# Input tiles first and in a row, decay loads and two sigmoids held back, GLA gate weights in two loads and copies

## The chip, the core and the metric

The kernel runs on one core of a Trainium2 chip. The metric is the device time of one execution in microseconds (us). The engines are TensorE (PE, matrix products, with its own weight loads), VectorE (DVE), ScalarE (ACT), GpSimd (POOL) and SyncE (SP), which only issues DMAs here. ACT issues DMAs as well, from the same queue as its arithmetic.

## What is computed

One step of a two-layer backbone over 128 context tokens and 512 latent tokens of width 1024. Layer 0 mixes with two groups of heads side by side, HGRN2 (4 heads) and GLA (4 heads of key width 64); layer 1 is retention with 8 heads. Every scan runs in both directions.

```python
def rms_norm(x, w):
    y = xf * lax.rsqrt(jnp.mean(xf * xf, axis=-1, keepdims=True) + EPS)
    return (y * w.astype(jnp.float32)).astype(x.dtype)
...
    for l in range(DEPTH):
        sh_c, sc_c, g_c = jnp.split(cond_ctx @ ada_w[l] + ada_b[l], 3, axis=-1)
        ...
        h_c = rms_norm(x_c, norm_w[l]) * (1.0 + sc_c) + sh_c
        h_l = rms_norm(x_l, norm_w[l]) * (1.0 + sc_l) + sh_l
        ...
# layer 0
    p = h @ w_in
    aq, ai, af_f, af_b, ag, bq, bk, bv, bg, bl_f, bl_b = jnp.split(p, EVEN_SPLIT_IDX, axis=-1)
    def log_forget(a):
        return jnp.logaddexp(jnp.log(lbf), jnp.log1p(-lbf) + jax.nn.log_sigmoid(a.astype(jnp.float32)))
    def gla_log_gate(low, d):
        return jax.nn.log_sigmoid((low @ gk_w[d] + gk_b[d]).astype(jnp.float32)) / GLA_GATE_NORM
# layer 1
    lg = jax.nn.log_sigmoid(decay_logit.astype(jnp.float32))
# every head: the scan
    S_t = diag(g_t) S_{t-1} + k_t v_t^T,  o_t = S_t^T q_t
```

`ret_decay` (the decay logits of layer 1), `hgrn_lb` (the lower bounds of layer 0's HGRN gate) and `gla_gk_w` (two 16x256 matrices, one per direction) are the small inputs that the change is about, beside `norm_w`, `gla_gk_b` and `ada_b`.

## The kernel before

**Staging.** PE's order is the order in which the program is written. The other engines' instructions are put in order by the framework's scheduler, except inside a `manual_schedule` block that names their engine, where the written order holds. `issue_after(ins)` keeps the instructions inside it behind `ins` on their engine. The program as built gives its hardware DMAs eight completion semaphores in turn, and a DMA waits in the queue that issues it until the one eight before it has landed.

**Front.** Five token tiles `x0` to `x4` (128x1024; the loads stand at L128 and L509) are normalised, scaled (`x_scaled`), transposed on PE (`pxt`) and copied to `xnt`. `ident` is the identity for transposes. `vrows` holds 76 rows of small vectors that ACT's queue loads in four pieces (L141 to L144 in the changed kernel); transposed and copied they are `vecs`. The adaLN weights of layer 0 come in chunks `ada` (two loads of 512 KB for each of eight steps k); each step k is a run of `pada` products on PE, a copy `arow` on ACT (L259), a transpose `padv` on PE (L89), small DVE operations on `ab`, and then `first_h(k)`, which makes `h0h` (ACT, L491) and `h0l` (DVE, L492), the two fp32 halves of the input of layer 0.

**Weights.** A block of 128x512 fp32 (256 KB) goes through three steps: SP loads `raw` (L171, five buffers), ACT casts it to `wh` (L180, eight buffers), and POOL, or DVE for a few, takes the difference `wl` (L182, eight buffers). `weights(i)` writes these for blocks ahead of use. A full-precision product is three matmuls, of `h` and `l` halves.

**The k loop** (`pbv`, GLA's values) runs over the eight steps k with the five tiles inside; `first_h(k + 1)` and the adaLN step k + 2 are written into it. At k = 5 the tile `gkw` (128x512, the two 16x256 matrices repeated in four row groups at places that depend on the direction) is cleared and loaded, and `wbl` too.

**Behind it.** `plow` (the low-rank projection) is copied by ACT to `low` (L574); `pz`, made with `gkw`, gives the GLA gates through a chain of ACT activations and DVE operations (L755 to L783) to `K` and `Q`, from which PE takes the scores `px`. `lbv` and `clb` are sigmoids of `hgrn_lb` for the HGRN gate. Then come two GLA head rows, with the projection of the HGRN values between them (`ids_ai`; ACT's copies `v`, L796), and the HGRN heads. In a row, ACT copies scores to `A` (L717, L718) and transposed keys to `kt` (L725), PE multiplies `pkv` from `v` and `kt`, and `po` is the output. `decays()` makes the tables of layer 1's decays: loads `lags` and `lag`, two `log_sigmoid` chains on the small tiles `lsb` and `lsr`, and `dk`, `tab`; they are read in layer 1.

Of the kernel before, what the change touches and what calls it, by code (L numbers as in the profile page):

```python
# [19 lines left out]
NT = 5  # L20
# [21 lines left out]
def hybrid_kernel(  # L42
# [20 lines left out]
    def ps(name="ps"):  # L63
        return psp.tile([128, 512], F32, tag="ps", name=name)
# [60 lines left out]

    ident = const.tile([128, 128], F32, name="ident")
    x_t = [tokt(f"x{t}") for t in range(NT)]
    SP.dma_start(x_t[0], x_rows[0])  # L128
    SP.dma_start(ident, k_ident)
    condr = const.tile([16, 128], F32, name="condr")  # L130
    nc.scalar.dma_start(condr[0:8, :], c_ctx.rearrange("(k p) -> k p", p=128))
    nc.scalar.dma_start(condr[8:16, :], c.rearrange("o (k p) -> (o k) p", p=128))
    NV = 76
    O_NW, O_LB, O_GKB, O_AB = (0, 8), 16, 24, (28, 52)
    vrows = const.tile([NV, 128], F32, name="vrows")
    ACTQ = nc.scalar
    ACTQ.dma_start(vrows[0:16, :], norm_w.rearrange("l (k p) -> (l k) p", p=128))
    ACTQ.dma_start(vrows[16:24, :], hgrn_lb.rearrange("l (k p) -> (l k) p", p=128))
    ACTQ.dma_start(vrows[24:28, :], gla_gk_b.rearrange("o d (k p) -> (o d k) p", p=128))
    ACTQ.dma_start(vrows[28:76, :], ada_b.rearrange("l (k p) -> (l k) p", p=128))  # L140
    mask = const.tile([128, 6, 64], U8, name="mask")  # L141
    mhalf = const.tile([128, 1], F32, name="mhalf")
    V.memset(mhalf, -0.5)
# [350 lines left out]
    def x_square(t):  # L494
        return rms(x_t[t], junk)
# [12 lines left out]
    for t in range(1, NT):
        SP.dma_start(x_t[t], x_rows[t])  # L509
    chunks = {0: ada_first(0)}  # L510
    weights(ids_bv[0], 0)
    chunks[1] = ada_first(1)
    weights(ids_bv[1], 0)
    chunks[2] = ada_first(2)
    with tc.manual_schedule(engines={mybir.EngineType.Activation, mybir.EngineType.DVE, mybir.EngineType.Pool}):
        p = ps("pv")
        transpose(p[:, 0:16], condr)
        S.activation(condp[:, :, 0:2], p[:, 0:16].rearrange("p (c k) -> p k c", c=2), AF.Silu)
        transpose(p[:, 128:128 + NV], vrows)
        V.tensor_copy(vecs, p[:, 128:128 + NV])  # L520
        for l in range(2):
            one = vecs[:, O_AB[l] + 8:O_AB[l] + 16]
            V.tensor_scalar(one, one, 1.0, None, op0=ADD)
        r = [x_square(t) for t in range(2)]
        x_scaled(0, r[0])
        for t in range(NT):
            if t + 1 < NT:
                x_scaled(t + 1, r[t + 1])
            if t + 2 < NT:
                r.append(x_square(t + 2))  # L530
            if t == NT - 1:
                fin = ada_first_mm(0, chunks[0])
                next(fin)
            x_turned(t)
        for _ in fin:
            pass
        first_h(0, 0)
        first_h(0, 1)
        fin = ada_first_mm(1, chunks[1])
        next(fin)  # L540
    pv = [ps(f"pbv{t}") for t in range(NT)]
    for k in range(KC):
        wh, wl = weights(ids_bv[k], 1 if k < 6 else LOOK)
        if k + 3 < KC:
            chunks[k + 3] = ada_first(k + 3)
        if k == 5:
            gkw = tokt("gkw")[:, 0:512].rearrange("p (d n) -> p d n", d=2)
            G.memset(gkw, 0.0)
            for gg in range(4):
                for d in range(2):  # L550
                    ACTQ.dma_start(gkw[32 * gg + 16 * d:32 * gg + 16 * d + 16, d, :], gla_gk_w[0, d])
            wbl = tokt("wbl")[:, 0:256].rearrange("p (k n) -> p k n", k=KC)
            ACTQ.dma_start(wbl, w0.rearrange("(k p) n -> p k n", p=128)[:, :, C_BL:C_BL + 32])
        for t in range(NT):
            g, o = group_of(t)
# [70 lines left out]
    def decays():  # L626
        lags = misc.tile([128, 20], F32, tag="lags", name="lags", bufs=1)
        lag = misc.tile([8, 257], F32, tag="lag", name="lag", bufs=1)
        zb, z8 = lags[:, 2:18], lags[0:8, 18:20]
        ACTQ.dma_start(zb, ret_decay.rearrange("o d h -> o (d h)").to_broadcast([128, 16]))  # L630
        ACTQ.dma_start(z8, ret_decay.rearrange("o d h -> (o h) d"))
        ACTQ.dma_start(lags[:, 0:2], k_ramp)
        ACTQ.dma_start(lag[:, 128:257], k_lag[:, 128:257])
        ACTQ.dma_start(lag[:, 0:128], k_lag[:, 257:385])
# [434 lines left out]
```

## Time and profile before

| | before |
|---|---|
| median of 3 runs | 795.43 us (794.30 to 798.55) |
| the profiled execution | 797.16 us |
| its span, first to last instruction | 795.4 us |
| mean granted PE clock, share of full speed | 0.984 |
| PE / DVE / ACT / POOL busy | 758.2 / 428.8 / 334.2 / 289.6 us |

Times of a row of the timeline are a start, counted from the span's start, and a duration. A number in brackets behind a row is the idle time of its engine just ahead of it and what ended it. In windows, x counts the instructions; the clock of 0.50 is 1.2 GHz, of 1.00 2.4 GHz. In the rows, L numbers are lines of the kernel before.

### The profile page before, as it was taken

How to read it: one execution, taken by the hardware profiler on the slowest of the kernel's cores; microseconds unless marked ns; L12 is line 12 of the kernel's file. 1: busy time of each engine (PE TensorE's matmuls, PEld its weight loads, DVE VectorE, ACT ScalarE, POOL GpSimd, SP SyncE). 2: the span in 40 equal slices, each digit the busy share in tenths (PEclk: the TensorE clock that was granted, in tenths of full speed). 3: DMA queues.
4: the chain of work that ended last, by engine and by line, in shares of the span. 5: the costliest groups of instructions: out<-in, count | busy, mean ns of one | idle time of the engine just before them, and what ended most of it. 6: DMA issues, size and time to landing. Idle time of an engine off the chain costs nothing.

```text
span 795.4 us, 15429 instructions
## 1 busy us (share of the span) xinstructions
PE 758.2 (95%) x6116; PEld 664.2 (84%) x6116; DVE 428.8 (54%) x744; ACT 334.2 (42%) x757; POOL 289.6 (36%) x263
## 2 busy tenths in 40 slices
PE   4999789999989899899999999999999999999996
PEld 3768778789889798778888888899999999888885
DVE  4973793752986666663444940036454646324433
ACT  6447643444534444443534552324333332235322
POOL 2261430265552522331344521544443532043221
PEclk9999899999999999999999999999999999999998
DMA  9982432364433431318524432334333333544003
GB/s 292 315 268 92 142 108 62 114 181 126 144 96 107 147 98 38 81 41 265 152 84 145 152 118 87 94 105 106 100 104 90 115 91 94 173 126 133 14 26 133
DMA packets 104776, 98.62 MB, mean 124 GB/s; under 512 B 7660, under 2 KB 80896, under 8 KB 104704
## 3 DMA queue, kind: packets, MB, share of 16 engines
q1 hardware_dynamic: 83520, 82.15, 33.4%
q10 hardware_dynamic: 21184, 15.49, 7.1%
q8 instruction: 48, 0.79, 0.4%
q14 instruction: 24, 0.20, 0.1%
HBM read 86.31 MB, written 8.16 MB: 119 GB/s over the span
## 4 chain that ended last, share of the span: by engine, by line
PE 68%; DVE 8%; issue 2%; ACT 1%; POOL 1%; DMA 1%; ACTq 0%; POOLq 0%; DVEq 0%
PE pt L85 32%; PE pf L85 21%; PE po L85 5%; PE px L85 4%; PE pkv L85 3%; DVE K L695 2%; DVE T L821 1%; DVE T L699 1%; PE pyt L89 1%; PE pada L85 1%; PE pkt L89 1%; DMA rot<-qk 1%; DVE K L819 1%; DVE Q L697 1%; PE pxt L89 1%
## 5 line engine op out<-in xcount | busy, mean ns | idle before, releaser
L182 POOL TENSOR_TENSOR wl<-raw,wh 128x512 fp32r<-128x512 f32 x142 | 203.0, 1444 | 309.4 <-ACT wh L180 264.4
L180 ACT CAST wh<-raw 128x512 fp32r<-128x512 f32 x168 | 103.2, 621 | 97.8 <-PE pf L85 37.0
L85 PE MATMUL pf<-h0h,wh 128*128 128x384 f32 (+1 forms) x256 | 64.1, 332 | 0.0
L335 DVE SCALAR_TENSOR_TENSOR y<-po,rr,gn 128x128 f32<-128x128 f32 x80 | 24.2, 345 | 72.3 <-POOL rr L158 60.5
L85 PE MATMUL pf<-h1h,wh 128*128 128x384 f32 (+1 forms) x256 | 60.3, 317 | 0.0
L85 PE MATMUL pf<-h0l,wh 128*128 128x384 f32 (+1 forms) x256 | 58.9, 311 | 0.0
L85 PE MATMUL pf<-h0h,wl 128*128 128x384 f32 (+1 forms) x256 | 58.6, 310 | 0.0
L85 PE MATMUL pf<-h1l,wh 128*128 128x384 f32 (+1 forms) x256 | 58.3, 309 | 0.0
L85 PE MATMUL pf<-h1h,wl 128*128 128x384 f32 (+1 forms) x256 | 58.3, 309 | 0.0
L687 ACT COPY km<-K 128x640 f32<-128x640 f32 x42 | 32.8, 782 | 56.3 <-DVE K L695 40.8
L85 PE MATMUL pt<-wh,h1h 128*128 128x512 f32 x160 | 53.9, 402 | 0.0
L156 POOL TENSOR_SCALAR rv<-ss 128x3 f32<-128x3 f32 (+1 forms) x32 | 11.0, 345 | 113.0 <-ACT junk L327 111.8
L85 PE MATMUL pt<-wh,h1l 128*128 128x512 f32 x160 | 52.1, 390 | 0.0
L85 PE MATMUL pt<-wl,h1h 128*128 128x512 f32 x160 | 52.0, 390 | 0.0
L697 DVE TENSOR_TENSOR Q<-Q,T 128x640 f32<-128x640 f32 x42 | 40.5, 964 | 19.2 <-PE px L85 19.1
L916 DVE TENSOR_TENSOR qk<-qk,cs 128x1024 f32<-128x1024 f32 x8 | 9.8, 1226 | 74.9 <-DMA rot<-qk 74.9
L695 DVE TENSOR_TENSOR K<-K,T 128x640 f32<-128x640 f32 x42 | 44.8, 1067 | 6.4 <-ACT km L687 5.9
L327 ACT ACTIVATE junk<-po 128x128 f32<-128x128 f32 x80 | 22.3, 278 | 54.0 <-PE po L85 41.7
L85 PEld LDWEIGHTS pf<-h0h,wh 128*128 128x128 f32 x256 | 39.6, 192 | 4.8 <-issue 2.3
L85 PE MATMUL pt<-wh,h0h 128*128 128x512 f32 x120 | 43.7, 429 | 0.0
L85 PEld LDWEIGHTS px<-Q,km 64*64 64x64 f32 (+1 forms) x1120 | 29.9, 139 | 15.7 <-issue 9.7
L85 PE MATMUL px<-Q,km 64*64 64x64 f32 (+1 forms) x1120 | 35.6, 231 | 5.9 <-DVE Q L697 4.8
(219 smaller groups left out, 1702.2 us busy)
## 6 DMA issues: line engine op xcount, KB each, us to landing
raw<-in_w_in_even_dram SPq DMA_DIRECT2D x64, 256.0 KB, 3.0
araw<-in_ada_w_dram SPq DMA_DIRECT2D x64, 256.0 KB, 3.7
raw<-in_w_in_odd_dram SPq DMA_DIRECT2D x64, 256.0 KB, 2.9
ada<-in_ada_w_dram SPq DMA_DIRECT2D x16, 512.0 KB, 6.3
raw<-in_w_out_even_dram SPq DMA_DIRECT2D x24, 256.0 KB, 3.0
rot<-qk ACTq DMA_DIRECT2D x32, 128.0 KB, 3.5
raw<-in_w_out_odd_dram SPq DMA_DIRECT2D x16, 256.0 KB, 3.0
x<-xr SPq DMA_DIRECT2D x5, 512.0 KB, 2.7
```

The lines of the kernel that those rows point to most:

```text
L85: PE.matmul(out, lhsT, rhs, **kw)
L89: PE.transpose(out, in_, ident[0:in_.shape[0], 0:in_.shape[0]])
L156: G.tensor_scalar(v[:, :n], ssum, 1.0 / count, EPS, op0=MUL, op1=ADD)
L180: S.copy(wh, raw)
L182: (V if n in on_dve else G).tensor_tensor(wl, raw, wh.bitcast(F32), op=SUB)
L327: S.activation(junk, p[:, 128 * i:128 * i + 128], AF.Square, accum_out=ss[:, j:j + 1])
L335: V.scalar_tensor_tensor(dst, p[:, 128 * i:128 * i + 128], r[:, j:j + 1], dst if have else gn[:, col:col + 128], op0=MUL, op1=MUL)
L687: S.copy(km.rearrange("p (n b h) -> p n b h", b=2, h=h), ap(kf, 0, ([2 * h, T // (2 * h)], [T + h, 2], [1, h])))
L695: V.tensor_tensor(keys, keys, ap(th, 1, ([nn - 1, 2], [2, nb], [0, h])), op=MUL)
L697: V.tensor_tensor(queries, queries, ap(th, 0, ([nn + 1, 2], [2, nb], [0, h])), op=MUL)
L699: V.tensor_tensor(t2, ap(th, 0, ([nn, 2], [2, nb])), ap(th, 1, ([nn, 2], [2, nb])), op=MUL)
L916: V.tensor_tensor(lat, lat, cos.unsqueeze(1).to_broadcast([128, 2, 512]), op=MUL)
```

## The change

Five edits. The x tiles, `ident` and `condr` are issued at the start inside a manual order for SP, and the four loads of `vrows` go from ACT's queue to SP's, behind them; the transpose of `vrows` goes to just ahead of the last but one x tile. The `ada` and first `raw` loads are in written order too. `gkw` is loaded in two pieces for the first row group, and POOL copies it to the three others. The two sigmoids of `lbv` are kept behind the last `low` copy. The five loads of `decays()` are kept behind the last `v` copy of the HGRN projection; what is worked out from them follows.

```diff
@@ start
-    SP.dma_start(x_t[0], x_rows[0])
-    SP.dma_start(ident, k_ident)
...
+    with tc.manual_schedule(engines={mybir.EngineType.SP}):
+        SP.dma_start(x_t[0], x_rows[0])
+        nc.scalar.dma_start(condr[0:8, :], c_ctx.rearrange("(k p) -> k p", p=128))
+        SP.dma_start(ident, k_ident)
+        nc.scalar.dma_start(condr[8:16, :], c.rearrange("o (k p) -> (o k) p", p=128))
+        for t in range(1, NT):
+            SP.dma_start(x_t[t], x_rows[t])
...
-    ACTQ.dma_start(vrows[0:16, :], norm_w.rearrange("l (k p) -> (l k) p", p=128))
...
+    with tc.manual_schedule(engines={mybir.EngineType.SP}):
+        SP.dma_start(vrows[0:16, :], norm_w.rearrange("l (k p) -> (l k) p", p=128))
...
@@ x tiles
+            if t == NT - 2:
+                pq = ps("pv")
+                transpose(pq[:, 0:NV], vrows)
+                V.tensor_copy(vecs, pq[:, 0:NV])
...
@@ k == 5
             G.memset(gkw, 0.0)
-            for gg in range(4):
-                for d in range(2):
-                    ACTQ.dma_start(gkw[32 * gg + 16 * d:32 * gg + 16 * d + 16, d, :], gla_gk_w[0, d])
+            for d in range(2):
+                ACTQ.dma_start(gkw[16 * d:16 * d + 16, d, :], gla_gk_w[0, d])
+            for gg in range(1, 4):
+                G.tensor_copy(gkw[32 * gg:32 * gg + 32], gkw[0:32])
@@ behind the k loop
-        S.copy(low[:, off:off + n], p[:, :n])
+        last_low = S.copy(low[:, off:off + n], p[:, :n])
...
-    S.activation(clb, lbv, AF.Sigmoid, scale=-1.0)
-    S.activation(lbv, lbv, AF.Sigmoid)
+    with tc.issue_after(last_low.ins):
+        S.activation(clb, lbv, AF.Sigmoid, scale=-1.0)
+        S.activation(lbv, lbv, AF.Sigmoid)
@@ decays
+        with tc.issue_after(copied[-1].ins):
+            ACTQ.dma_start(zb, ret_decay.rearrange("o d h -> o (d h)").to_broadcast([128, 16]))
...
+            ACTQ.dma_start(lag[:, 0:128], k_lag[:, 257:385])
...
     def v_use(t, p):
-        S.copy(v_t[t][:, 0:512], p)
+        copied.append(S.copy(v_t[t][:, 0:512], p))
```

What stands on ACT at the end of the first GLA head row, before the change (`pt` is the product of the values' projection, `px` the scores, `pkt` the transposed keys):

```order
L796 COPY v_752<-pt 128x512
L717 COPY A<-px 64x5x64
L718 COPY A<-px 64x5x64
L717 COPY A<-px 64x5x64
L718 COPY A<-px 64x5x64
L725 COPY kt<-pkt 128x512 x2
L180 CAST wh<-raw 128x512
```

and after it (lines are those of the changed kernel, where L725 and L726 are the `A` copies and L733 the `kt` copies):

```order
L806 COPY v_759<-pt 128x512
L638 DMA lags<-in_ret_decay_dram 128x16
L639 DMA lags<-in_ret_decay_dram 8x2x1
L640 DMA lags<-in_k_ramp_dram 128x2
...
L641 DMA lag<-in_k_lag_dram 8x129
L642 DMA lag<-in_k_lag_dram 8x128
L606 ACTIVATE lsb<-lags 128x16
L607 ACT_TABLE_LOAD
L607 ACTIVATE lsb<-lsb 128x16
L733 COPY kt<-pkt 128x512 x2
L184 CAST wh<-raw 128x512
```

Between the `v` copy and the `kt` copies now stand five DMA issues, two activations and a table load; the four `A` copies, left out here, keep their place between the third and the fourth issue. The second `lag` issue waits for the semaphore of a weight block's `raw` load.

What stands on ACT behind the `low` copies, ahead of GLA's gates, before:

```order
L574 COPY low<-plow 128x256
L574 COPY low<-plow 128x384
L665 DMA S<-in_state_gla_dram 128x128
L755 ACTIVATE Q<-pz,vecs 128x256
L665 DMA S<-in_state_gla_dram 128x128
L755 ACTIVATE Q<-pz,vecs 128x384
```

and after:

```order
L580 COPY low<-plow 128x256
L580 COPY low<-plow 128x384
L589 ACT_TABLE_LOAD
L589 ACTIVATE clb<-lbv 128x4
L763 ACTIVATE Q<-pz,vecs 128x256
L590 ACTIVATE lbv<-lbv 128x4
L763 ACTIVATE Q<-pz,vecs 128x384
```

A table load and the two sigmoids have come in, ahead of and between the first `Q` activations. In the whole program ACT loads a table 18 times instead of 17.

What stands on ACT around k = 5 to 7 of the k loop, before (`pada` is the adaLN product of a step, `xnt` the transposed tiles):

```order
L553 DMA wbl<-in_w_in_even_dram 128x8x32
L180 CAST wh<-raw 128x512
L551 DMA gkw<-in_gla_gk_w_dram 16x256 x4
L491 CAST h0h_111<-xnt_109 128x256
L551 DMA gkw<-in_gla_gk_w_dram 16x256
L491 CAST h0h_113<-xnt_109 128x384
L259 COPY arow<-pada 128x128
L180 CAST wh<-raw 128x512
L551 DMA gkw<-in_gla_gk_w_dram 16x256 x3
L180 CAST wh<-raw 128x512 x3
L491 CAST h0h_111<-xnt_109 128x256
```

and after:

```order
L559 DMA wbl<-in_w_in_even_dram 128x8x32
L184 CAST wh<-raw 128x512
L555 DMA gkw<-in_gla_gk_w_dram 16x256 x2
L495 CAST h0h_121<-xnt_119 128x256
L495 CAST h0h_123<-xnt_119 128x384
L263 COPY arow<-pada 128x128
L184 CAST wh<-raw 128x512 x5
L495 CAST h0h_121<-xnt_119 128x256
L184 CAST wh<-raw 128x512
L495 CAST h0h_123<-xnt_119 128x384
L263 COPY arow<-pada 128x128
```

Two `gkw` issues stand where eight stood, in one place, and five casts instead of four, and a sixth, stand ahead of the last `h0h` and `arow` shown. On POOL the copies stand between the clearing of `gkw` and the next differences:

```order
L553 MEMSET gkw 128x512
L557 COPY gkw<-gkw 32x512 x2
L186 TENSOR_TENSOR wl<-raw,wh 128x512
L557 COPY gkw<-gkw 32x512
L186 TENSOR_TENSOR wl<-raw,wh 128x512 x11
```

Before, the clearing of `gkw` was followed by eleven differences and nothing between.

## Rows read from the trace of the kernel before

**Rows 1.** The page's busy times by engine, of the whole span
```profile
PE 758.2 (95%) x6116; PEld 664.2 (84%) x6116; DVE 428.8 (54%) x744; ACT 334.2 (42%) x757; POOL 289.6 (36%) x263
```

**Rows 2.** Windows: busy us by engine, PE's clock, DMA share, GB/s
```profile
5.00:8.00 3.00, 0.36 (x1) 0.18 (x1) 0.76 (x6) 2.97 (x5) 0.42 (x2) 1.00 0.64 155
...
12.00:28.00 16.00, 14.40 (x164) 10.64 (x167) 14.11 (x50) 9.37 (x26) 4.44 (x7) 1.00 1.13 348
```

**Rows 3.** Waits of SP, 0 to 13 us: us, times, longest
```profile
SPq L509 <- DMA vrows<-in_norm_w_dram: 2.8, 1, 2.8
```

**Rows 4.** Timeline of PE, 19 to 24 us: start, us; in brackets idle before
```profile
19.25 1.07 PE L85 MATMUL pada<-ada,condp 128*32 128x128 f32 x28 [0.94 <-DMA ada<-in_ada_w_dram]
```

**Rows 5.** Timeline of PE, 54.5 to 57 us
```profile
55.20 0.50 PE L85 MATMUL pbv<-wh,h0h 128*128 128x512 f32 x1 [1.07 <-ACT h0h L491]
...
56.58 0.50 PE L85 MATMUL pbv<-wh,h0l 128*128 128x512 f32 x1 [0.88 <-DVE h0l L492]
```

**Rows 6.** Windows in which PE's clock was 0.50
```profile
57.30:60.50 3.20, 3.20 (x10) 2.43 (x9) 2.61 (x4) 0.00 (x0) 1.92 (x2) 0.50 0.62 176
...
238.20:241.40 3.20, 3.20 (x40) 2.50 (x38) 2.99 (x10) 0.05 (x1) 0.00 (x0) 0.50 0.39 93
```

**Rows 7.** Timeline of PE, 236.8 to 240 us
```profile
236.85 2.65 PE L85 MATMUL pkv<-v,kt 128*128 128x128 f32 x16 [2.20 <-ACT kt L725]
```

**Rows 8.** Timeline of ACT, 65 to 69 us
```profile
65.47 2.02 ACT L755 ACTIVATE Q<-pz,vecs 128x384 f32<-128x384 f32 x4 [0.41 <-PE pz L85]
...
67.51 1.28 ACT L757 ACT_TABLE_LOAD   x1
...
68.81 1.28 ACT L757 ACTIVATE Q<-Q 128x1280 f32<-128x1280 f32 x1
```

**Rows 9.** Timelines of DVE at 81 us and of PE at 95 us
```profile
81.21 1.49 DVE L765 SCALAR_TENSOR_TENSOR Q<-T,Q 128x1280 f32<-128x1280 f32 x1 [5.63 <-ACT Q L764]
...
95.14 0.92 PE L85 MATMUL px<-q,K 64*64 64x64 f32 x24 [2.94 <-DVE K L783]
```

**Rows 10.** Timelines of SP, ACT and PE, 166 to 173 us
```profile
166.82 0.37 SPq L171 DMA_DIRECT2D raw<-in_w_in_even_dram  x1
...
169.40 1.07 ACT L725 COPY kt<-pkt 128x512 f32<-128x512 f32 x2 [0.96 <-PE pkt L89]
...
170.62 1.97 PE L85 MATMUL pkv<-v,kt 128*64 128x128 f32 x32
```

**Rows 11.** Timeline of DVE, 25 to 26 us
```profile
25.09 0.59 DVE L610 SCALAR_TENSOR_TENSOR lsb<-lsb 128x16 f32<-128x16 f32 x3
```

**Rows 12.** Timeline of PE, 27 to 39 us, the adaLN steps
```profile
27.68 1.08 PE L85 MATMUL pada<-ada,condp 128*32 128x128 f32 x32
...
32.75 1.08 PE L85 MATMUL pada<-ada,condp 128*32 128x128 f32 x32
...
37.52 1.08 PE L85 MATMUL pada<-ada,condp 128*32 128x128 f32 x32
```

**Rows 13.** Waits of ACT, 36 to 50 us
```profile
ACT h0h L491 <- DMA gkw<-in_gla_gk_w_dram: 1.9, 1, 1.9
```

**Rows 14.** DMA issues, 36 to 50 us: count, KB each, us to landing
```profile
wbl<-in_w_in_even_dram ACTq DMA_DIRECT2D x1, 128.0 KB, 5.4
...
gkw<-in_gla_gk_w_dram ACTq DMA_DIRECT2D x8, 16.0 KB, 3.9
```

**Rows 15.** Timelines of ACT at 39 us and of PE at 51 us
```profile
39.28 0.26 ACT L259 COPY arow<-pada 128x128 f32<-128x128 f32 x1
...
51.03 0.27 PE L89 MATMUL padv<-ident,arow 128*128 128x128 f32 x1
```

**Rows 16.** The page's groups (busy, mean ns, idle before) and DMA issues
```profile
L182 POOL TENSOR_TENSOR wl<-raw,wh 128x512 fp32r<-128x512 f32 x142 | 203.0, 1444 | 309.4 <-ACT wh L180 264.4
...
L180 ACT CAST wh<-raw 128x512 fp32r<-128x512 f32 x168 | 103.2, 621 | 97.8 <-PE pf L85 37.0
...
raw<-in_w_in_even_dram SPq DMA_DIRECT2D x64, 256.0 KB, 3.0
```

More of the change, by code (lines that the diff above doesn't have):

```diff
@@ L127, in hybrid_kernel @@
     x_t = [tokt(f"x{t}") for t in range(NT)]
-    SP.dma_start(x_t[0], x_rows[0])
-    SP.dma_start(ident, k_ident)
     condr = const.tile([16, 128], F32, name="condr")
-    nc.scalar.dma_start(condr[0:8, :], c_ctx.rearrange("(k p) -> k p", p=128))
-    nc.scalar.dma_start(condr[8:16, :], c.rearrange("o (k p) -> (o k) p", p=128))
+    with tc.manual_schedule(engines={mybir.EngineType.SP}):
[5 more added lines that the diff above has]
+            SP.dma_start(x_t[t], x_rows[t])
     NV = 76
@@ L136, in hybrid_kernel @@
     ACTQ = nc.scalar
-    ACTQ.dma_start(vrows[0:16, :], norm_w.rearrange("l (k p) -> (l k) p", p=128))
-    ACTQ.dma_start(vrows[16:24, :], hgrn_lb.rearrange("l (k p) -> (l k) p", p=128))
-    ACTQ.dma_start(vrows[24:28, :], gla_gk_b.rearrange("o d (k p) -> (o d k) p", p=128))
-    ACTQ.dma_start(vrows[28:76, :], ada_b.rearrange("l (k p) -> (l k) p", p=128))
+    with tc.manual_schedule(engines={mybir.EngineType.SP}):
+        SP.dma_start(vrows[0:16, :], norm_w.rearrange("l (k p) -> (l k) p", p=128))
+        SP.dma_start(vrows[16:24, :], hgrn_lb.rearrange("l (k p) -> (l k) p", p=128))
+        SP.dma_start(vrows[24:28, :], gla_gk_b.rearrange("o d (k p) -> (o d k) p", p=128))
+        SP.dma_start(vrows[28:76, :], ada_b.rearrange("l (k p) -> (l k) p", p=128))
     mask = const.tile([128, 6, 64], U8, name="mask")
@@ L506, in x_turned @@
                                                 p.rearrange("p (k n) -> p k n", k=4))
[L508 to L514, printed above, removed]
+    with tc.manual_schedule(engines={mybir.EngineType.SP}):
+        chunks = {0: ada_first(0)}
+        weights(ids_bv[0], 0)
+        chunks[1] = ada_first(1)
+        weights(ids_bv[1], 0)
+        chunks[2] = ada_first(2)
     with tc.manual_schedule(engines={mybir.EngineType.Activation, mybir.EngineType.DVE, mybir.EngineType.Pool}):
@@ L518, in hybrid_kernel @@
         S.activation(condp[:, :, 0:2], p[:, 0:16].rearrange("p (c k) -> p k c", c=2), AF.Silu)
[L519 to L523, printed above, removed]
         r = [x_square(t) for t in range(2)]
@@ L530, in hybrid_kernel @@
                 r.append(x_square(t + 2))
+            if t == NT - 2:
+                pq = ps("pv")
+                transpose(pq[:, 0:NV], vrows)
+                V.tensor_copy(vecs, pq[:, 0:NV])
+                for l in range(2):
+                    one = vecs[:, O_AB[l] + 8:O_AB[l] + 16]
+                    V.tensor_scalar(one, one, 1.0, None, op0=ADD)
             if t == NT - 1:
@@ L629, in decays @@
         zb, z8 = lags[:, 2:18], lags[0:8, 18:20]
[L630 to L634, printed above, removed]
+        with tc.issue_after(copied[-1].ins):
+            ACTQ.dma_start(zb, ret_decay.rearrange("o d h -> o (d h)").to_broadcast([128, 16]))
+            ACTQ.dma_start(z8, ret_decay.rearrange("o d h -> (o h) d"))
+            ACTQ.dma_start(lags[:, 0:2], k_ramp)
+            ACTQ.dma_start(lag[:, 128:257], k_lag[:, 128:257])
+            ACTQ.dma_start(lag[:, 0:128], k_lag[:, 257:385])
         lg = misc.tile([128, 16], F32, tag="lg", name="lg", bufs=1)
@@ L792, in hybrid_kernel @@
                    new_gla[0, 0, :, 2 * r:2 * r + 2].rearrange("d h k v -> (h k) d v"), y_t, gn), D_GLA)
+    copied = []
     def v_use(t, p):
-        S.copy(v_t[t][:, 0:512], p)
+        copied.append(S.copy(v_t[t][:, 0:512], p))
     run(proj_tm(ids_ai, act, v_use))
```

## The prediction

> **What bounds the kernel now.** I read the page first. TensorE (PE) is busy for 95% of the span and every other engine for little more than half of it or less [rows 1], so an edit to another engine's work counts only where PE stands still for it, or where a standstill lowers PE's clock. The whole of PE's idle time is 5% of 795.4 us, some 37 us, and the change touches four stretches of it, so I went on to the windows, the waits and PE's own timeline in those four.
>
> The first is the start. Between 5 and 8 us the DMA engines moved 155 GB/s, between 12 and 28 us 348 GB/s [rows 2]; in the gap SP stood for 2.8 us on a load of `vrows` that another queue had issued [rows 3]. Later PE waits 0.94 us for an `ada` load, ahead of the second adaLN step [rows 4]: what the transfers lost in the gap arrives at PE there.
>
> The second is the end of the k loop, at 55 us. PE stands 1.07 us for `h0h` and 0.88 us for `h0l` [rows 5], and then runs 3.2 us at a granted clock of 0.50, 1.2 GHz instead of 2.4 [rows 6]. The same table has a second such stretch, at 238 us, and it too follows a standstill, of 2.20 us for a `kt` copy [rows 7]. In these two places a wait of about 2 us cost a second time through the clock, 3.2 x 0.50 = 1.6 us.
>
> The third is GLA's gate chain. ACT works through the `Q<-pz` activations with only 0.41 us of idle time, and then loads a table [rows 8]. DVE waits 5.63 us for what comes out of ACT, and PE 2.94 us for what comes out of DVE [rows 9]. ACT, DVE and PE are one chain here: time added to ACT between `low` and the gates shows up at PE.
>
> The fourth is the first GLA head row's end at 169 us, where PE's `pkv` begins 1.22 us after ACT began the `kt` copies [rows 10], with no wait noted at PE. There is no slack to speak of in that copy.
>
> **The sum is made against one execution.** Its span is 795.4 us, its time 797.16; it lies 1.73 us above the median of the runs, 795.43. A measurement of this kernel tells some 0.5%, 3.98 us, from no change: below 791.45 is faster, above 799.41 slower.
>
> **Loads in a row.** x1 to x4 no longer stand behind `vrows`. The bytes that the gap lost are 3.0 us x (348 - 155) GB/s = 0.58 MB, at 348 GB/s 1.67 us. Everything that SP issues behind them, the `ada` chunks too, comes that much earlier, and because PE waited for one of them [rows 4] I take all of it: **-1.67 us**. Bounds: nothing, if the four small loads take on SP's queue what they gave up on ACT's, and -2.8 us, the whole wait [rows 3]. The `vrows` loads now land behind x4, and their transpose stands just ahead of x3's. That costs nothing while the scaling of x3 on DVE ends after they land; where it ends first, PE loses up to the 0.94 us that it can spare there now [rows 4].
>
> **Decay chain out of the front.** Some 38 small DVE operations leave the first 35 us; three of them took 0.59 us [rows 11], so 0.2 us each. They stood between the `first_h` operations. Two adaLN steps of PE apart, with them the distance was 32.75 - 27.68 = 5.07 us, after them 37.52 - 32.75 = 4.77 us [rows 12]. One step gains the difference: **-0.3 us**. Bounds: 0, if the transfers set the pace of these steps, and -0.9, three steps of it.
>
> **GLA gate weights.** ACT's queue no longer stands on eight `gkw` loads; its longest such wait was 1.9 us, ahead of an `h0h` [rows 13]. I take it to be where the late work at k = 7 came from. But POOL now waits for the landing, 3.9 us after the issue [rows 14], and makes two copies before its next `wl` (the difference of a weight block), which gives SP the buffer for the next raw block, and ACT's cast of that block stands, as the orders show, ahead of the `h0h` of k = 6 and the `arow` of k = 7. Step by step, in the time of before and with 2.0 us taken off for the front: the last `arow` ahead of it at 39.28 + 0.26 - 2.0 = 37.5 [rows 15]; a cast, 0.62 [rows 16], and the issue at 38.1; landing 42.0; two copies to 43.3; the `wl` at 1.3 to 44.6; the raw load, 3.0 [rows 16], to 47.6; cast 0.62, `h0h` as much as a cast, `arow` 0.26: 49.1. PE takes that `arow` at 51.03 - 2.0 = 49.0 [rows 15]. A 32x512 copy on POOL stands nowhere in the trace. Its price lies between ACT's cast of the same width, 0.62, and POOL's own `wl` with two operands, 1.44 on average [rows 16]; I take 0.65, since it reads one operand as the cast does. So the new chain arrives within 0.1 us of when it is needed, ACT's old wait is gone, and a wait of the same size can stand at the same place. I forecast **0** for this part. Bounds: -3.55, if the 1.07 + 0.88 us standstill and its 1.6 us of half clock go, and +3.1, if the chain is 1.5 us late and lowers the clock once more.
>
> **Sigmoid of `lbv` behind `low`.** A table load of 1.28 us [rows 8] and two activations on 128x4, which I price at 0.2 us each by DVE's small operations [rows 11], now stand on ACT ahead of or among the `Q<-pz` activations. 1.28 + 0.4 less 0.41 of idle time is **+1.27 us**, and the chain through DVE carries it to `px`, whose wait grows from 2.94 to 4.2 us. Bounds: 0, if PE's `pz` came later than ACT can take it, and +1.7.
> On the way into such a load and out of it the row shows no pause: the operation ahead of it ends at 67.49, the load runs from 67.51 to 68.79, and the next activation starts at 68.81 [rows 8].
> The Trainium skill, page "ScalarE: Activation LUTs", section "What ACT_TABLE_LOAD costs", gives about 1283 ns for the load and adds about 1380 ns of draining for every switch. The trace agrees on the load alone; with the page's drain at both places where a load is new, the sum would be 2 x 1.38 = 2.76 us higher.
>
> **Decays at the row's end.** They now follow the last `v` copy. On ACT two of their loads and two activations with a table load come straight ahead of the `kt` copies. Each DMA of the program waits in its queue for the one eight before it, and the second `lag` load has a raw weight block before it, which was issued at 166.82 [rows 10] and lands 3.0 later, at 169.8. ACT therefore stands there until 169.8, issues (0.37 by the row of SP), does an Abs (0.2), loads the table (1.28) and does a sigmoid (0.2): 171.9. The first `kt` takes half of 1.07, so PE's `pkv` can begin at 172.4 to 172.5 instead of 170.62: **+1.9 us**. Bounds: 0, if the issue finds its semaphore set (the chain behind it, some 2.0 us, then runs in ACT's idle time and little of it reaches `kt`), and +4.3, if the raw block takes as long to land as `wbl` did, 5.4 us instead of 3.0 [rows 14, 16]. What stands behind the wait on ACT is a `wh` cast and DVE's remaining decay work; PE has its `pkv`, `pf` and first `po` in front of those, which hides them.
> A standstill of 1.9 us is about that of [rows 5] and [rows 7], and both were followed by 3.2 us of half clock: **+1.6 us**; bounds 0 and 1.6.
>
> **Sum:** -1.67 - 0.3 + 0 + 1.27 + 1.9 + 1.6 = +2.8 us, 797.16 + 2.8 = 799.96, less the 1.73 by which that execution stood above the median: **798.2 us**.
>
> **The rivals.**
> A, the forecast, 798.2: all as summed. Chance 0.38. With the bounds of the loads (a gain of 0 to 2.8) it covers 797 to 800.
> B, the row's standstill comes but the clock holds: 796.6. For it: 1.9 us is the smallest of the three waits. 0.13.
> C, the k = 7 bunch goes and its half clock with it: 798.2 - 3.55 = 794.7. For it: ACT's wait of 1.9 us was the one removed. Against it: the chain through POOL has no slack. 0.17.
> D, slower: the `gkw` copies come late. The two loads are 16 KB pieces like the eight, but `wbl`, issued just ahead, took 5.4 us against 3.9 [rows 14]; if `gkw` lands with it, POOL, the raw block and `arow` are 1.5 us late, PE waits for `padv`, and the clock falls once more: 798.2 + 1.5 + 1.6 = 801.3. It decides as soon as `gkw` lands more than 3.9 us after its issue, or each copy takes over 0.65. 0.20.
> E, faster: C holds and the `lag` load finds its semaphore set, so that neither the wait at `kt` nor its half clock comes: 794.7 - 3.5 = 791.2. 0.10.
> F, a pause as long as the load itself stands at each of the two new table loads: 798.2 + 2 x 1.28 = 800.8. Against it: the load in [rows 8] has none on either side. 0.02. It is the drain of which the Trainium skill speaks on the page named above.
>
> **Range and chances.** The likeliest is A, 798.2. With E and the larger gain of the loads the low end is 790.5 (791.2 less the half of the 1.1 us between 1.67 and 2.8); with D and half of what the `kt` wait can be longer, 801.3 + 1.2, the high end is 802.5; some 2 in 10 lie outside. Faster by over 0.5% are most of E and a quarter of C, 0.14. Slower are D, F and the upper third of A, 0.33. Within 0.5% is the rest, 0.53.
>
> **What would show it.** Front: no gap in DMA between 5 and 8 us, `pada` steps 1.7 us earlier, no wait for `ada`. k = 7: a wait of PE for `padv` or `h0h`, and whether a stretch of half clock follows. Gates: a table load right behind the `low` copies, and `px` waiting 4.2 us. Row's end: ACT idle up to about 170 us ending on a DMA, a table load before `kt`, PE waiting about 1.9 us at `pkv`, and a clock of 0.50 behind it. The prediction is wrong if ACT's `lag` issues don't wait, if PE had other work during the `kt` delay, or if DVE was late in the gate chain for a reason of its own.

## The result, and the profile after

The changed kernel takes 801.25 us (median of 10 runs, 798.71 to 803.31), the kernel before 795.04 us (10 runs, 793.17 to 798.55): a ratio of 1.0076, 95% interval 1.0059 to 1.0094, or 4.7 to 7.5 us more. It is slower. The prediction had said 798.2, in a range of 790.5 to 802.5, with a chance of 0.33 for slower.

The page of the changed kernel, span and busy times:

```profile
span 798.0 us, 15428 instructions
...
PE 758.5 (95%) x6116; PEld 666.0 (83%) x6116; DVE 430.7 (54%) x744; ACT 336.2 (42%) x758; POOL 292.3 (37%) x266
```

PE's busy time has grown by 0.3 us [rows 1]; what was lost is waiting. PE's order is the same in both kernels but for one transpose, so the start of one and the same instruction in both traces shows where it was lost (one execution each). At the adaLN step that began at 32.75 us [rows 12] the changed kernel is 0.39 us late, at `px` [rows 9] 1.18 us, at the first row's `pkv` [rows 10] 4.77 us.

**The front.** Windows of the changed kernel (columns as in [rows 2]):

```profile
5.00:8.00 3.00, 0.29 (x2) 0.30 (x3) 0.75 (x1) 0.94 (x2) 0.75 (x2) 1.00 0.96 321
12.00:28.00 16.00, 14.59 (x149) 11.56 (x148) 10.15 (x29) 7.26 (x16) 4.22 (x6) 1.00 1.04 308
0.00:20.00 20.00, 10.75 (x95) 9.30 (x99) 8.73 (x23) 10.50 (x19) 5.58 (x15) 1.00 0.92 289
```

and one of the kernel before:

```profile
0.00:20.00 20.00, 9.54 (x105) 7.70 (x107) 9.78 (x30) 12.89 (x28) 5.56 (x15) 1.00 0.91 293
```

The gap between 5 and 8 us is filled, 321 GB/s for 155 [rows 2]. But from 12 to 28 us the transfers run at 308 GB/s instead of 348, and over the first 20 us as a whole they moved 289 GB/s, before 293. SP's waits up to 13 us and SP's first issue of the second `ada` pair, changed kernel:

```profile
SPq L470 <- DMA x<-in_x_sample_dram: 2.8, 2, 1.9
```

```profile
11.96 1.64 SPq L470 DMA_DIRECT2D ada<-in_ada_w_dram  x2
```

The wait of 2.8 us on `vrows` [rows 3] has become 2.8 us on the x tiles, in two waits, ahead of the `ada` loads. The second pair goes out at 11.96 us; before, it did at 12.36. PE's timeline in the changed kernel:

```profile
10.95 3.68 PE L89 MATMUL pxt<-ident,x 128*128 128x128 f32 x16 [1.27 <-DVE x L502]
...
14.54 1.92 PE L89 MATMUL pxt<-ident,x 128*128 128x128 f32 x8
...
17.55 1.09 PE L89 MATMUL pxt<-ident,x 128*128 128x128 f32 x8
...
19.62 1.07 PE L85 MATMUL pada<-ada,condp 128*32 128x128 f32 x28 [0.53 <-DMA ada<-in_ada_w_dram]
...
33.14 1.08 PE L85 MATMUL pada<-ada,condp 128*32 128x128 f32 x32
```

The second adaLN step still waits for `ada`, 0.53 us, and begins at 19.62, before at 19.25 [rows 4].

**The k loop.** Timelines of PE, POOL and DVE, changed kernel:

```profile
51.11 0.50 PE L85 MATMUL pbv<-wh,h0h 128*128 128x512 f32 x1 [0.30 <-ACT h0h L495]
53.45 0.50 PE L85 MATMUL pbv<-wh,h0l 128*128 128x512 f32 x1 [1.84 <-DVE h0l L496]
...
45.39 1.74 POOL L557 COPY gkw<-gkw 32x512 f32<-32x512 f32 x2 [7.76 <-DMA gkw<-in_gla_gk_w_dram]
...
48.54 3.45 DVE L492 TENSOR_SCALAR xnt<-xnt,ab 128x128 f32<-128x128 f32 x3
51.91 3.04 DVE L496 TENSOR_TENSOR h0l<-xnt,h0h 128x256 fp32r<-128x256 f32 x2
```

and the window behind the standstill:

```profile
54.30:57.60 3.30, 3.30 (x9) 2.52 (x9) 3.19 (x7) 0.00 (x0) 3.02 (x3) 0.50 1.05 351
```

PE stands 2.14 us at k = 6 instead of 1.95 us at k = 7 [rows 5], and one stretch of half clock follows as before [rows 6]. POOL had stood 7.76 us for `gkw` and then worked without a break; beside it the three DVE operations that make the input of k = 6 took 3.45 us, and the two differences `h0l` behind them 3.04. The same three before, and POOL's wait before:

```profile
47.37 1.00 DVE L488 TENSOR_SCALAR xnt<-xnt,ab 128x128 f32<-128x128 f32 x3
...
46.02 1.29 POOL L182 TENSOR_TENSOR wl<-raw,wh 128x512 fp32r<-128x512 f32 x1 [7.78 <-ACT wh L180]
```

So POOL had stood as long before the change, 7.78 us, for ACT's cast, which stood in the queue with the eight `gkw` issues; a burst of POOL's work behind that wait is in both kernels.

**The gates.** Timelines of ACT and PE, changed kernel:

```profile
64.44 0.48 ACT L580 COPY low<-plow 128x384 f32<-128x384 f32 x1 [0.92 <-PE plow L85]
64.94 1.28 ACT L589 ACT_TABLE_LOAD   x1
66.23 0.21 ACT L589 ACTIVATE clb<-lbv 128x4 f32<-128x4 f32 x1
68.59 1.28 ACT L765 ACT_TABLE_LOAD   x1
...
96.32 0.92 PE L85 MATMUL px<-q,K 64*64 64x64 f32 x24 [3.66 <-DVE K L791]
```

The table load stands where it was foreseen, and `px` waits 3.66 us instead of 2.94. Behind `px` PE's clock is at 0.50 in both kernels, for 6.8 us before and 10.2 us after; the prediction doesn't mention this stretch. Its extra 3.4 us cost next to nothing: from `px` to `pkv` PE takes 75.48 us before and 79.07 after, of which 3.40 are the wait at `pkv`.

**The first row's end.** Timelines of SP, ACT and PE, changed kernel:

```profile
168.15 0.37 SPq L175 DMA_DIRECT2D raw<-in_w_in_even_dram  x1
...
171.97 0.30 ACTq L641 DMA_DIRECT2D lag<-in_k_lag_dram  x1
172.64 0.29 ACTq L642 DMA_DIRECT2D lag<-in_k_lag_dram  x1
172.98 0.21 ACT L606 ACTIVATE lsb<-lags 128x16 f32<-128x16 f32 x1 [3.22 <-DMA raw<-in_w_in_even_dram]
173.22 1.28 ACT L607 ACT_TABLE_LOAD   x1
174.51 0.22 ACT L607 ACTIVATE lsb<-lsb 128x16 f32<-128x16 f32 x1
174.75 1.07 ACT L733 COPY kt<-pkt 128x512 f32<-128x512 f32 x2
...
175.39 1.97 PE L85 MATMUL pkv<-v,kt 128*64 128x128 f32 x32 [3.40 <-ACT kt L733]
```

ACT does no arithmetic for 3.22 us, the wait ends on a raw block, and PE stands 3.40 us for `kt`. Both `lag` issues stand, not the second alone: ACT's last `A` copy ended at 169.76, the first issue goes at 171.97 and the second at 172.64, 4.5 us after the `raw` issue at 168.15. Behind it, where half clock was foreseen:

```profile
175.40:178.60 3.20, 3.20 (x41) 3.03 (x42) 2.11 (x8) 1.41 (x5) 1.28 (x1) 1.00 0.52 171
```

the granted clock stayed at 1.00, 2.4 GHz. The two profiled executions differ once more behind this, in a stretch that the change doesn't touch: before,

```profile
279.20:282.40 3.20, 3.20 (x16) 3.20 (x15) 3.03 (x8) 0.00 (x0) 0.40 (x1) 0.50 0.28 82
```

and after it

```profile
283.60:286.80 3.20, 3.20 (x27) 3.20 (x27) 3.06 (x7) 0.06 (x1) 0.82 (x1) 1.00 0.26 82
```

PE is 4.8 us late ahead of it and 3.7 behind it, and by 601 us, in layer 1, 2.6, by which the spans differ too. Sums are therefore made up to `pkv`.

### The profile page after: what moved, and what is told of

The parts are those of the page before. It is cut to its first block, busy times and chain, and to the rows that moved or that the text cites. A ratio compares the mean times of both kernels' runs of the same rounds, so it can differ in the third digit from the quotient of the medians.

```text
span 798.0 us, 15428 instructions
## 1 busy us (share of the span) xinstructions
PE 758.5 (95%) x6116; PEld 666.0 (83%) x6116; DVE 430.7 (54%) x744; ACT 336.2 (42%) x758; POOL 292.3 (37%) x266
## 4 chain that ended last, share of the span: by engine, by line
PE 69%; DVE 8%; issue 2%; ACT 1%; POOL 1%; DMA 0%; POOLq 0%; ACTq 0%; DVEq 0%
PE pt L85 32%; PE pf L85 22%; PE po L85 5%; PE px L85 4%; PE pkv L85 3%; DVE K L703 2%; DVE T L707 1%; DVE T L831 1%; PE pyt L89 1%; PE pada L85 1%; PE pkt L89 1%; DVE K L829 1%; DVE Q L705 1%; PE pxt L89 1%; ACT wh L184 0%
## 5 line engine op out<-in xcount | busy, mean ns | idle before, releaser
L186 POOL TENSOR_TENSOR wl<-raw,wh 128x512 fp32r<-128x512 f32 x142 | 200.5, 1427 | 304.0 <-ACT wh L184 257.7
```

The lines of the kernel that those rows point to most:

```text
L186: (V if n in on_dve else G).tensor_tensor(wl, raw, wh.bitcast(F32), op=SUB)
```

## The experiments

Medians stand beside those of the kernel before on the same chip; intervals are of the ratio. The changed kernel was 6.2 us over the kernel before; kernels built on it are compared with it by what each has over the kernel before.

### One part of the change alone

**p_decay**: only the hold on the decay loads.

```diff
+        with tc.issue_after(copied[-1].ins):
             ACTQ.dma_start(zb, ret_decay.rearrange("o d h -> o (d h)").to_broadcast([128, 16]))
```

> Of the change, only the five decay loads held behind the last v copy. Theory 1 (the slow-down is made at the end of the first GLA head row, where ACT stands on its lag issues until raw blocks have landed): PE waits 3 to 4 us for kt there, as the 3.40 us in the changed kernel, and little is gained in the front; +3 to +5 us, 798 to 800. Theory 2 (the parts are each near nothing and only their meeting moves the clock's stretches): within 1 us of before.

799.84 us beside 795.86, 1.0061 (1.0038 to 1.0085). PE waits at the row's end as in the changed kernel:

```profile
173.93 1.97 PE L85 MATMUL pkv<-v,kt 128*64 128x128 f32 x32 [3.13 <-ACT kt L726]
```

Theory 1 holds: this one edit costs 4.0 us by the medians (3.0 to 6.8), with everything else as before. The loads stand as before here, and yet the gap of the front is filled, 323 GB/s between 5 and 8 us, and PE's second adaLN step begins at 18.91, the step of 32.75 at 33.19.

**p_front**: only the order of the input tiles and `vrows`.

```diff
+        for t in range(1, NT):
+            SP.dma_start(x_t[t], x_rows[t])
...
+        SP.dma_start(vrows[0:16, :], norm_w.rearrange("l (k p) -> (l k) p", p=128))
```

> Of the change, only the order of the input tiles and vrows. Theory 1 (SP's wait on vrows is replaced by its wait of 2.8 us for x tiles ahead of the ada loads, and PE's adaLN steps come 0.5 us later as in the changed kernel): 0 to +1 us. Theory 2 (the front is gained as predicted, and another part hid it in the changed kernel): -1 to -2 us.

801.10 us beside 795.86, 1.0072 (1.0049 to 1.0094). Both theories fall; alone, the new order costs 5 us. Timelines of PE and ACT in it:

```profile
11.25 1.97 PE L89 MATMUL pxt<-ident,x 128*128 128x128 f32 x8 [6.58 <-DVE x L502]
...
6.73 0.22 ACT L604 ACTIVATE lsb<-lags 128x16 f32<-128x16 f32 x1 [1.00 <-DMA lags<-in_ret_decay_dram]
6.97 1.28 ACT L521 ACT_TABLE_LOAD   x1
8.26 0.19 ACT L521 ACTIVATE condp<-pv 128x16 f32<-128x16 f32 x1
```

With `vrows` gone from ACT's queue, the decay loads and the first activation of their chain come first on ACT; the squares of the x tiles wait for them and for two table loads, and PE's first transposes begin at 11.25 us (7.7 in the changed kernel). So the hold on the decays isn't separate from the new order: it takes away a cost that the new order creates.

**p_gkw**: only the two loads and three copies of `gkw`.

```diff
+            for d in range(2):
+                ACTQ.dma_start(gkw[16 * d:16 * d + 16, d, :], gla_gk_w[0, d])
+            for gg in range(1, 4):
+                G.tensor_copy(gkw[32 * gg:32 * gg + 32], gkw[0:32])
```

> Of the change, only gkw in two loads and three POOL copies. Theory 1 (POOL waits for the landing, its differences then come in a bunch and slow DVE's first_h operations; the standstill moves from k = 7 to k = 6 and stays as long): within 1 us of before, with a wait of PE at h0l and one stretch at 0.50 in the k loop. Theory 2 (removing eight issues from ACT's queue gains and another part took it back): -2 to -3.6 us, no such stretch.

797.68 us beside 795.86, 1.0016 (0.9997 to 1.0035): no gain, and not told from nothing. PE stands 1.81 us for `h0l` at k = 6 and another 2.02 us for `h0h` at k = 7, with one stretch at 0.50 behind the second; `px` comes at 97.22, 2.1 us later than before. Theory 1 is the nearer, though it had one standstill and at most 1 us.

**p_sig**: only the two sigmoids behind `low`.

```diff
+    with tc.issue_after(last_low.ins):
         S.activation(clb, lbv, AF.Sigmoid, scale=-1.0)
```

> Of the change, only the two sigmoids held behind low. Theory 1 (ACT, DVE and PE are one chain at the gates): px waits 0.7 to 1.3 us longer than 2.94, and the front gains nothing from the table load that it loses: +0.5 to +1.3 us. Theory 2 (the front is bound by ACT's squares, and the table load that leaves it is worth 1.3 us there): -0.6 to 0 us.

795.72 us beside 795.86, 1.0000 (0.9980 to 1.0021). `px` waits 3.08 us, 0.14 longer than before. Neither theory had the reason: this kernel has no table load between the `low` copies and the sigmoids, and 17 loads in all; the load that stood with the sigmoids in the front stands there now with the decay chain's sigmoid, at 17.37 us. The table load at the gates comes only where both edits meet.

### The changed kernel with one thing undone or moved

**a_early**: without the hold on the decay loads.

```diff
-        with tc.issue_after(copied[-1].ins):
```

> The changed kernel without the hold on the decay loads. Theory 1 (the decay chain in front is what costs the new order of the loads 5 us when it stands alone; the hold takes that away and costs 3 us at the row's end): PE's first x transposes start near 11.3 us as with the loads' order alone, no wait of 3 us for kt; 800 to 803. Theory 2 (the hold costs 3 to 5 us and the rest next to nothing): 796 to 798.

802.02 us beside 795.67, 1.0078 (1.0056 to 1.0100). The `kt` wait is gone, and PE's first x transposes begin at 11.87 us. Theory 1: without the hold `px` comes at 102.07, 5.75 us later than in the changed kernel; with it `kt` costs 3.40 us at the row. Both are read from two traces; by the medians, 6.35 and 6.2 us over the kernel before, the hold gains nothing that can be told.

**a_lag**: the two `lag` loads held further back, the rest of the decays where the change put them.

```diff
+        with tc.issue_after(last_af[0].ins):
             ACTQ.dma_start(lag[:, 128:257], k_lag[:, 128:257])
             ACTQ.dma_start(lag[:, 0:128], k_lag[:, 257:385])
```

> The changed kernel with only the two lag loads held further back, behind the last HGRN gate activation; the three lags loads, the log-sigmoid and its table load stay at the end of the first GLA row. Theory 1 (most of PE's 3.40 us at kt is ACT standing on the raw blocks' landing ahead of these two issues): the wait falls to 0.5 to 1.5 us and the time by about 2 us, to 798.5 to 800. Theory 2 (it is the table load, the two activations and the lags' own landing): the wait stays at 2.5 us or more, time within 1 us of the changed kernel.

799.86 us beside 795.67, 1.0056 (1.0037 to 1.0075). Timelines of PE and ACT:

```profile
173.20 1.97 PE L85 MATMUL pkv<-v,kt 128*64 128x128 f32 x32 [1.80 <-ACT kt L734]
...
170.46 0.22 ACT L606 ACTIVATE lsb<-lags 128x16 f32<-128x16 f32 x1 [1.14 <-DMA lags<-in_ret_decay_dram]
170.69 1.28 ACT L607 ACT_TABLE_LOAD   x1
```

PE's wait fell from 3.40 to 1.80 us, between the two theories. By these two traces standing on the raw blocks is worth 1.6 us; the landing of `lags`, the table load and the activations, four here ahead of `kt` instead of two, make up the rest. The size is not firm: four other kernels with the row's end of the changed kernel (p_decay, a_gkw2, a_ada, a_warm) have waits of 3.13, 3.10, 2.84 and 2.06 us there.

**a_late**: all five decay loads held behind the last HGRN gate activation.

```diff
-        with tc.issue_after(copied[-1].ins):
+        with tc.issue_after(last_af[0].ins):
```

> The changed kernel with all five decay loads held behind the last HGRN gate activation, where ACT has the sigmoid table loaded. Theory 1: no wait at the first GLA row's kt, one table load fewer; what is left over before is 0.5 us of the front and 0.7 us of the gates: 796 to 798. Theory 2 (the loads and their chain cost as much wherever they stand, by a wait at the HGRN kt): 799 to 802.

799.60 us beside 795.67, 1.0062 (1.0039 to 1.0084). No wait at the first row, but a new one in the last HGRN row:

```profile
322.30 1.44 PE L85 MATMUL pkv<-v,kt 128*128 128x128 f32 x8 [1.87 <-ACT kt L733]
...
321.58 0.20 ACT L607 ACTIVATE lsr<-lsr 8x2 f32<-8x2 f32 x1 [3.23 <-DVE lsb L614]
321.69 0.56 ACT L733 COPY kt<-pkt 128x512 f32<-128x512 f32 x1
```

An `lsr` sigmoid waits 3.23 us on ACT for the chain's own DVE operations, and `kt` is queued behind it. Theory 2, though by another path than a load's.

**a_gkw2**: `gkw` cleared, loaded and copied at k = 2.

```diff
-        if k == 5:
+        if k == 2:
             gkw = tokt("gkw")[:, 0:512].rearrange("p (d n) -> p d n", d=2)
```

> The changed kernel with gkw cleared, loaded and copied at k = 2 instead of k = 5. Theory 1 (POOL, held 7.8 us for the landing of gkw, then does its differences in a bunch and slows DVE): POOL's wait is gone, no wait for h0l at k = 6 or 7 and no clock of 0.50 in the k loop; 3 to 3.6 us less than the changed kernel, 797.5 to 798.5. Theory 2 (the bunch comes from the jump of the weights' look-ahead at k = 6): a wait of 1 to 2 us and the half clock remain, time within 1 us of the changed kernel.

800.21 us beside 795.67, 1.0058 (1.0038 to 1.0077). In the k loop the clock stays at 1.00 and there is no wait for `h0l`, as theory 1 said; but PE waits 0.70 us for a `wl` at 42.1 and 0.20 and 1.05 us for `h0h`, nearly the 2.14 us of the changed kernel. The time is 4.5 us over the kernel before instead of 6.2, with intervals that overlap; the clock now fell behind the `kt` wait. PE's timeline and the window:

```profile
174.09 3.18 PE L85 MATMUL pkv<-v,kt 128*64 128x128 f32 x29 [3.10 <-ACT kt L734]
```

```profile
173.40:176.60 3.20, 2.51 (x24) 2.51 (x26) 0.74 (x4) 1.94 (x6) 1.27 (x1) 0.51 0.79 250
```

**a_ada**: the four `vrows` loads behind the first two `ada` loads.

```diff
         chunks = {0: ada_first(0)}
+        SP.dma_start(vrows[0:16, :], norm_w.rearrange("l (k p) -> (l k) p", p=128))
...
```

> The changed kernel with the four vrows loads behind the first two ada loads on SP. Theory 1 (the ada loads are late because SP must have x tiles landed before it may issue them, the four vrows loads having used up the free semaphores): the ada loads are issued 2 to 3 us earlier than at 7.97 us, PE's wait of 0.5 us for ada goes and the adaLN steps come 1 to 1.7 us earlier than in the changed kernel; 799.5 to 800.3. Theory 2 (the x chain through ACT, POOL and DVE sets the front): steps within 0.5 us of the changed kernel, time within 1 us.

800.61 us beside 795.93, 1.0070 (1.0053 to 1.0087). The first `ada` pair is issued at 3.54 us instead of 7.97, the second at 12.42, and the second adaLN step begins at 19.50 us with a wait of 1.01 us for `ada`. Theory 1 falls: SP's wait for the x tiles was not what kept the steps from coming earlier. 4.4 us of earlier issue brought PE's second step 0.12 us.

**a_warm**: 19 transposes on PE that nobody reads, while it waits for the first and the second x tile.

```diff
+        for i in range(14):
+            transpose(warm[:, 128 * (i % 4):128 * (i % 4) + 128], ident)
```

> The changed kernel with 19 transposes of ident on PE that nobody reads, 14 while it waits for the first x tile and 5 while it waits for the second. Theory 1 (in the changed kernel PE does its x transposes at half pace, 0.42 us each, up to 16.7 us, because it stood still ahead of them; before, up to 13 us): the x transposes reach 0.27 us each by 12 us, the first adaLN step starts at 15 to 15.7 us instead of 16.39, and the adaLN steps and the whole come 0.5 to 1.5 us earlier; 799.7 to 800.8. Theory 2 (the adaLN steps are set by the landing of the ada loads): transposes faster, wait for ada longer, steps and time within 0.5 us of the changed kernel.

801.46 us beside 795.62, 1.0079 (1.0062 to 1.0095). PE's timeline:

```profile
10.77 1.09 PE L89 MATMUL pxt<-ident,x 128*128 128x128 f32 x8
...
14.79 1.08 PE L85 MATMUL pada<-ada,condp 128*32 128x128 f32 x32
...
19.48 1.07 PE L85 MATMUL pada<-ada,condp 128*32 128x128 f32 x28 [1.00 <-DMA ada<-in_ada_w_dram]
...
24.38 1.07 PE L85 MATMUL pada<-ada,condp 128*32 128x128 f32 x28 [1.42 <-DMA ada<-in_ada_w_dram]
```

Eight transposes take 1.09 us from the second tile on, the first adaLN step begins 1.6 us earlier, and the second stands and waits for `ada`: 19.48 for 19.62. Theory 2.

### Tries at a version that beats both

**b_gkw2**: the kernel before with `gkw` in two loads and copies at k = 2; the diff is that of a_gkw2.

> The kernel before with gkw in two loads and copies, but at k = 2. Theory 1 (POOL's bunch at k = 6 and 7, from waiting for gkw, causes the standstill of 2 us and the half clock in the k loop): both go, -2 to -3.5 us, 792 to 793.5. Theory 2 (the standstill there returns for another reason, or the half clock only moves to the next standstill, as it did in the changed kernel with gkw at k = 2): -1 to 0 us.

795.61 us beside 795.93, 0.9991 (0.9976 to 1.0006). The clock was 1.00 throughout the end of the k loop, with waits of 0.44 and 1.05 us for `h0h`. In its profiled execution PE began the x transposes 2.4 us later than before, as DVE stood 8.6 us on a `lags` load at the start; the median gains nothing that can be told from noise, at most 1.9 us: theory 1's mechanism, theory 2's time.

**best2**: input tiles in a row, `vrows` behind the first `ada` pair, `gkw` at k = 2, sigmoids and decay loads behind a `first_h` cast of k = 1.

```diff
+        with tc.issue_after(first_cast[3].ins):
             ACTQ.dma_start(zb, ret_decay.rearrange("o d h -> o (d h)").to_broadcast([128, 16]))
```

> Input tiles in a row, vrows behind the first two ada loads, gkw at k = 2, the two sigmoids and the decay loads behind a first_h cast of k = 1, where ACT has time. Theory 1 (each cost that the runs have located is taken away: the SP wait, POOL's bunch, the table load at the gates, the decays at a row's end): front -1 to -1.7, k loop -2 to -3.5 against the kernel before; 790.5 to 793. Theory 2 (the small DVE operations in the k loop and the decay loads among the ada loads cost what is gained): 794.5 to 797.

797.54 us beside 795.93, 1.0027 (1.0012 to 1.0041): faster than the changed kernel by its median, slower than the one before by 0.1 to 0.4%. The decay chain now stands in the k loop; PE waits there

```profile
42.87 0.50 PE L85 MATMUL pbv<-wh,h0h 128*128 128x512 f32 x1 [1.77 <-ACT h0h L492]
```

and a stretch at 0.50 follows from 44.7 us. Theory 2, 0.5 us over its range. No kernel of the study can be told to be faster than the one before.

## Why the prediction came out as it did

The range held the time, and the mechanism of the largest term was right; one term failed, two were mis-sized, and one, the half clock, was not there in the profiled execution. That the range held is partly luck: the forecast, A, covered 797 to 800, and the high end of 802.5 came from rival D's price of 3.1 us, which was not paid. Step by step, in the prediction's order:

- **Loads in a row, -1.67.** Failed: nothing was gained. The step of 32.75 us came at 33.14, and at 32.71 to 32.82 in three kernels with the same front (a_lag, a_late, a_gkw2), so the +0.4 is within what executions differ by. The step that failed is "I take all of it": bytes that a gap loses are not late at PE when the later loads take the time back. SP issues the second `ada` pair at 11.96, 12.36 and 12.42 us in the changed kernel, the one before and a_ada, and the second adaLN step waits for `ada` and begins at 19.62, 19.25 and 19.50. Faster transposes (a_warm) and earlier first `ada` loads (a_ada) changed next to nothing there, nor did a filled gap without the new order (p_decay). Why the transfers run at 308 GB/s instead of 348 from 12 us on was not settled.
- **Decay chain out of the front, -0.3.** Right for the step it was read from. Its distance is 4.77 us, 28.37 to 33.14, in the changed kernel and in all six others without the chain there (p_decay, a_lag, a_late, a_gkw2, a_ada, a_warm); with the chain and the loads as before it is 5.07, and 5.43, 5.54 and 5.76 in p_gkw, p_sig and b_gkw2. At the end of the front the gain doesn't show: p_decay, which has this part alone, was 0.4 us late at the same step, not early. What the hold is worth was missed: p_front and a_early show some 5 us that it saves the new order of loads. The prediction took the parts one by one against the kernel before, where that cost doesn't exist, so its sum was not harmed.
- **GLA gate weights, 0.** Right in size in this trace (+0.07 at `px`), not in kind; alone, in p_gkw, the part made `px` 2.1 us late. The path of the prediction, raw block to cast to `arow`, was not what PE waited for: `arow` was done at 52.70 and PE took it at 54.02 without a wait. `gkw` was there 5.3 us after its issue at 40.12 instead of 3.9, two copies took 1.74 us instead of 1.3, and the wait moved from k = 7 to k = 6, for `h0l`, with one stretch of half clock. This is rival D's cause, with its threshold passed, but not its price: the new wait took the place of the old one and was not added to it. That 801.3 was D's number is chance. What slows the loop is POOL's burst of work after its wait, beside which DVE's three operations take 3.45 instead of 1.00 us; p_gkw shows the same, and a_gkw2 (`gkw` earlier, a shorter burst) 2.90 us. The Trainium skill, page "GPSIMD Engine Reference", section "1. Specifications", says that GpSimd's SBUF interfaces are shared with VectorE, with contention for VectorE's instructions in a 2-port perf mode or with two SBUF inputs; the `h0l` differences, which have two, agree, with 3.04 us beside the burst and 1.06 us ahead of it, at 43.76. In which mode the three operations with one input ran no run shows, and none took the sharing apart by itself.
- **Sigmoid behind `low`, +1.27.** Right in mechanism, too large: 3.66 - 2.94 = +0.72, and the other kernels with this load agree (3.65 to 3.70 in a_lag, a_late, a_gkw2, a_ada, a_warm). From the end of the `low` copies to the next table load ACT took 3.04 us before (64.47 to 67.51) and 3.67 after (64.92 to 68.59): more of the new work than the 0.41 us of the sum ran in time that ACT had to spare. p_sig shows that the cost hangs on the table load, which comes only when the decay chain has left the front. A pause around the load (rival F) is not there: it ends at 66.22 and the next activation begins at 66.23.
- **Decays at the row's end, +1.9.** Right in mechanism, mis-sized: +3.40. The term took 3.0 us for the landing of a raw block, the page's median over the whole run. In this place of the trace of before the blocks need more; its DMA issues from 165.3 to 167.2 us:

```profile
raw<-in_w_in_even_dram SPq DMA_DIRECT2D x2, 256.0 KB, 4.5
```

  With 4.5 the same sum gives 1.9 + 1.5 = 3.4. So good a fit holds for this pair of traces only: in p_decay, a_gkw2, a_ada and a_warm the same wait was 2.06 to 3.13 us, and a_lag, without standing on raw blocks, measured 1.80.
- **Half clock behind it, +1.6.** Not in the changed kernel's profiled execution, where 3.40 us of standstill were followed by a clock of 1.00, which is rival B's condition; but in a_gkw2's, after 3.10 us. Of the six kernels with a wait of 1.80 us or more at this `pkv` it is the only one with such a stretch behind it. The step that failed is taking two places where half clock followed for a rule; which of the two a given run has, the medians can't say.

Up to `pkv` the trace accounts for 0.39 + 0.07 (k loop) + 0.72 + 3.40 + 0.19 (small differences) = 4.77 us. The medians differ by 6.2, interval 4.7 to 7.5, and the two traces are not of median executions: that of the kernel before took 797.16 us, 2.1 over its median, that of the changed kernel 799.77, 1.5 under its own. The part over 4.77 is not located; a clock that falls behind the `kt` wait in some runs would give up to 1.6 of it, which is argued and not shown.

## What to carry to other kernels

A gap in the transfers is worth something only if the load that PE waits for next lands earlier: look for that, not for the bytes, nor for the issue alone; here the load left 0.40 us earlier and PE had it 0.37 us later. A DMA issue on an engine that also computes can stand on another queue's landing, and everything written behind it stands too; price that with the landing time of the very stretch, not with the run's median. And when parts of a change are taken alone, one of them may cost more than the whole, because another was made to mend it.

## What was not expected of the hardware

- In the changed kernel PE does eight x transposes in 1.92 us at 14.54 and in 1.09 us at 17.55, while the windows' clock column says 1.00 for both. The trace's record of the clock begins only at 16.75 us there, and at 12.85 before, so that the 1.00 ahead of it is no measurement. The kernel before has eight in 1.09 us already at 14.66:

```profile
14.66 1.09 PE L89 MATMUL pxt<-ident,x 128*128 128x128 f32 x8 [0.38 <-DVE x L498]
```

  With 19 idle transposes ahead of them (a_warm) they took 1.09 us from 10.77 on, and the time was the same.
- Beside POOL's burst in the changed kernel a DVE operation took 0.7 to 1.1 us longer whatever its size: 1.24 us for 128x2 elements at 47.26 (0.16 at 42.48), 1.08 on average for 128x128 at 48.54 (0.35 in the kernel before), 1.64 for a difference of 128x384 at 53.32 (0.56 at 44 us). One of POOL's own differences takes 1.28. That each DVE operation waits for one of POOL's to end is argued from these sizes and not shown.
- Stretches of half clock come and go between executions of the same work: the profiled execution of before has one at 238 [rows 6] and one at 279 us, that of the changed kernel one at 242 but none at 283.6, that of p_sig a mean clock of 1.00 in both places. Of the fourteen profiled executions twelve have the first and eight the second. At 3.2 x 0.5 = 1.6 us each they are as large as most terms of this case, so a single profiled time says little about a change of 2 us.
